# A hybrid decoder layer on one core: the small matrix products of the two token mixers, regrouped

## The chip, the cores and the metric

The kernel runs on one core of a Trainium2 chip. The metric is the device time of one execution in microseconds (us), lower is better; the times are medians over several runs. The core has a matrix engine (PE, whose weight loads are shown as PEld), a vector engine (DVE), a scalar engine (ACT), a general one (POOL), and queues that issue transfers (here almost all on SP).

## What is computed

One layer with two parallel token mixers, for 256 tokens (S) of 1024 channels, all in float32:

```python
n = rms_norm(h, norm1_g)
mq, mk, mv, gq, gk, gv, g_low, g_out, gate_moba, gate_gla = split(n @ w_in)
# MoBA: 8 heads of 64, one block of 256 keys: causal softmax attention
l_own = q @ k.T * scale + bias_hb[:, t5_bucket(d_own)]        # relative position bias
# GLA: 4 heads, dk = 128, dv = 256, chunks of 64 tokens
log_a = log_sigmoid(g_low @ gla_gate_up + gla_gate_bias) / 16  # g_low has 16 columns
attn = where(causal, (q * exp(b)) @ (k * exp(-b)).T, 0)        # b: cumulative sum of log_a in a chunk
mixed = sigmoid(gate_moba) * (y_moba @ w_branch_moba) + sigmoid(gate_gla) * (y_gla @ w_branch_gla)
h = h + mixed @ w_out
h = h + square(relu(rms_norm(h) @ w_up)) @ w_down
```

The weights are float32 and are read once; 78.74 MB are moved in all.

## The kernel before

**The large products.** Every large float32 product is made of three products of parts: an operand is split into a high part that is rounded to the type `float32r` and the low rest, and high x high, high x low and low x high are summed up in a PSUM bank. The weights come in units of 1 MB (`load`, L81). For each half of a unit ACT writes the high part (`wh`, L94) and, one step later, DVE the low part (`wl`, L98); when a unit's last low part is written, the transfer of the unit four further on is issued (L101). All of this runs two units ahead of PE (`split(hu + 2, ...)`). `block` (L118 to L120) multiplies 128 tokens by 512 columns, 4 x 3 products with 512 moving columns; `block_w` (L136 to L138) makes transposed results, 8 x 3 products with 256.

**The mixers' steps.** The projection is 26 units, each in two blocks; block number t of unit hu is slot 2 hu + t. A table of `at(slot, function)` (from L665) puts a small step of the mixers behind the slot's block. In every slot the order is written out: the block on PE, then `flush` (the deferred DVE halves of the slot before), then ACT's half of a weight split, then the results of the block, then the steps of the table in the order in which they were entered. Engines take their instructions in that order; nothing reorders them between engines. The results of the first two units (`mq`, `mk`) are entered as steps of slots 5 to 8, behind the table's own.

**The steps that the change touches:**
- `make_bias` (slot 7): one float32 product of 33 rows (32 buckets and a mask row), weights of 8 columns (`t5`) and 384 moving columns (`onehot`), both straight from transfers; bank `pbias`, L262. DVE copies the result (L264) and a transfer through memory spreads it.
- `g_diag`, `g_row` (slots 6 and 8): diag(rstd) by DVE (L459), then ones^T diag as one float32 product with 256 columns (bank `prow`, L466): the tokens' rstd in every row.
- `g_low` (slot 11): the 16 columns of the low-rank gate in 16 products with 256 columns; the weights `lowS` hold high, low, high, low parts, 64 columns (bank `plow`, L475 and L476). The result is split again into `lowHL`, 64 rows (L478 to L484).
- `g_decay` (two halves, slots 13 and 14): for each head 64 rows of `gup`'s high part by all of `lowHL` (L494), plus 32 rows of its low part by `lowHL`'s first 32 rows (L495), 256 columns each, bank `pz`.
- `m_transpose` (L316), `m_ptrans` (L395): four 128x128 transposes each on PE; `m_scores` (L326): for a pair of heads, which lie in rows 0 to 63 and 64 to 127, three products of parts for the one and then three for the other.
- `g_scores` (slots 38, 39): plain float32, for each head three products of a 128x128 tile of attention: L566 (all 128 keys by the first 64 queries), L567 (64 weight columns: the first chunk's keys by the last 64 queries) and L569 (64 weight columns: the second chunk's keys by the last 64 queries).

A plain float32 product is two MATMUL records in the profile, a `float32r` one is one. The names `128*64` in a row give rows x columns of the weights.

Of the kernel before, what the change touches and what calls it, by code (L numbers as in the profile page):

```python
# [19 lines left out]
S = 256  # L20
# [14 lines left out]
# Projection columns in units of 512, by their place in w_in, in the order that they are worked on.  # L35
# [6 lines left out]
# Columns of the packed per-partition vectors.  # L42
# [4 lines left out]
def block_kernel(ctx, tc, xT0_d, xT_d, x_d, vec_d, wlow_d, w_d, up_d, t5_d, onehot_d, out_d):  # L47
# [28 lines left out]
    # ---- weights: raw, then an exact split into two parts of 12 bits  # L76
# [26 lines left out]
    # The vector engine's half of a split is issued a step after the scalar engine's.  # L103
# [18 lines left out]
    def block_t(i, j, g, a, acc):  # L122
        """A transposed block: 128 columns of a unit that holds 256 for all of K, half of K, all tokens.
        The result is the sum of the bank's halves: those of the high and of the low parts in a."""
        for k in range(4):
            h, c = divmod(4 * g + k, 2)
            c = slice(c * 256 + j * P, c * 256 + (j + 1) * P)
            nc.tensor.matmul(acc, wH[i][:, h, c], a[:, k, :], start=g == 0 and k == 0, stop=False)  # L128
            nc.tensor.matmul(acc[:, S:], wL[i][:, h, c], a[:, k, :S], start=False, stop=g == 1 and k == 3)  # L129

    def block_w(i, j, g, aH, aL, acc):
        """The same, with the sum in one place."""
# [10 lines left out]
    # ---- first loads  # L143
# [19 lines left out]
    nc.vector.memset(t5[NB:NB + 1, :], 1.0)  # L163
    gup = mid("gup")
    ones = const.tile([P, P], F32, name="ones")
    nc.vector.memset(ones, 1.0)
    touch = const.tile([P, 1], F32, name="touch")
    nc.scalar.activation(touch, ones[:, 0:1], AF.Exp)

    # The tensor engine's clock rises while it works: keep it at work until the operands arrive.  # L170
# [18 lines left out]
    # ---- x^T times the gain, split  # L189
# [11 lines left out]
    def rsqrt(dst, ss, n):  # L201
        """dst = (ss / n + EPS) ** -0.5"""
# [15 lines left out]
    for r in range(4):  # L218
        nc.sync.dma_start(gup[16 * r:16 * r + 16, :], up_d)
# [19 lines left out]
    # The low-rank weights' columns: high, low, high, low parts; those that raise the rank: four copies  # L239
    T = {}  # L240
    lowS = const.tile([P, 8, 64], F32R, name="lowS")

    def low_split():
        v = lowS.rearrange("p k (r a c) -> p k r a c", r=2, a=2)
        for r in range(2):
# [4 lines left out]
    def gup_split():  # L250
        both = big("gupHL", F32R)
        T["gupH"], T["gupL"] = gupH, gupL = both[:64, :512], both[:32, 512:]
        nc.scalar.activation(gupH, gup[:64, :], AF.Copy)
        nc.vector.tensor_tensor(gupL, gup[:32, :], gupH[:32, :].bitcast(F32), op=OP.subtract)

    # ---- relative position bias: u[h, j] is the bias at distance 255 - j; bias[p, h, k] that of
    # query 128 + p and key k, which serves both tiles of queries
    bias = t4.tile([P, H, 256], F32, name="bias", tag="t8", bufs=2)

    def make_bias():  # L260
        pb = axbank("pbias")
        nc.tensor.matmul(pb[:H, :384], t5, onehot, start=True, stop=True)  # L262
# [5 lines left out]
    def spread_bias():  # L268
        """A copy for each partition, so that the row of partition p can start p elements earlier."""
# [13 lines left out]
    # ---- MoBA: one block of keys, so each query attends over its own block  # L283
# [40 lines left out]
    def m_scores(o, r, k, tq, tk):  # L324
        for i, (a, b) in enumerate(PARTS):
            nc.tensor.matmul(o, T["mq" + a][r, k, tq], T["mk" + b][r, k, tk], start=i == 0, stop=i == 2)  # L326

    def m_scores0():
        T["s0"] = big("s0").rearrange("p (k a c) -> p k a c", k=4, a=2)
        banks = [axbank(f"ps0{a}") for a in range(2)]  # L330
        for k in range(4):
            for a in range(2):
                r = slice(a * DH, (a + 1) * DH)
                m_scores(banks[a][:, k * P:(k + 1) * P], r, k, slice(0, P), slice(0, P))
# [5 lines left out]
    def m_scores1(half):  # L340
# [3 lines left out]
        for k in range(2):  # L344
            for a in range(2):
                r = slice(a * DH, (a + 1) * DH)
                m_scores(banks[a][:, k * S:(k + 1) * S], r, 2 * half + k, slice(P, S), slice(0, S))
# [25 lines left out]
    def m_weights(part):  # L373
        """The softmax's weights, from the exponentials."""
# [8 lines left out]
    def m_ptrans(part):  # L383
        """Transposes of the weights: heads 0-3 or 4-7 of query tile 0 (parts 0, 1), then of query
        tile 1 and keys 0-127 or 128-255 (parts 2-5)."""
# [24 lines left out]
    def m_av(k):  # L410
        """Of a pair of heads, transposed: both heads' values by each head's weights; the even head's
        result is in the upper rows of its columns, the odd head's in the lower ones."""
# [22 lines left out]
    def put_split(dH, dL, t, p, gain=None):  # L435
        """Splits a bank of four transposed tiles into the two parts, times a gain per row."""
# [18 lines left out]
    # ---- GLA  # L455
    def g_diag():
        T["diag"] = mid("diag")
        for t in range(NT):
            nc.vector.tensor_scalar(T["diag"][:, t * P:(t + 1) * P], ident, rstd[:, t:t + 1], None, op0=OP.mult)  # L459
# [3 lines left out]
    def g_row():  # L463
        """rstd of each token in all rows: ones^T diag(rstd)"""
        pr = axbank("prow")
        nc.tensor.matmul(pr[:, :S], ones, T["diag"][:, :S], start=True, stop=True)  # L466
        nc.scalar.activation(rrow, pr[:, :S], AF.Copy)

    def g_low():
        """The low-rank projection, transposed: rows 0-15 and 16-31 add up to it, and are there twice."""  # L470
        p = axbank("plow")
        o = p[:64, :S]
# [4 lines left out]
        low = mid("low")[:64, :S]  # L477
        nc.vector.tensor_tensor(low, o, rrow[:64, :], op=OP.mult)  # L478
        # Rows 0-31: the high part; rows 32-63: the low part
        both = t2.tile([P, 512], F32R, name="lowHL", tag="t2")  # L480
# [523 lines left out]
```

## Time and profile before

| | |
|---|---|
| median of 3 runs | 423.07 us (422.81 to 423.31) |
| the profiled execution: span from first to last instruction | 421.4 us |
| its own time beside the span | not recorded; the median is 1.67 us above the span |
| PE busy | 416.3 us, 99% of the span, 2160 products |
| PEld / DVE / ACT / POOL busy | 83% / 67% / 53% / 4% |
| mean granted clock of PE | 0.999 |
| transfers | 78.74 MB, 187 GB/s over the span |

Busy is the share of the span in which an engine had an instruction under way. Products overlap on PE, so a product's duration is longer than the time that it adds: what it adds is the distance from its start to the start of the next. Starts are the first number of a timeline row.

### The profile page before, as it was taken

The page shows a single profiled execution, that of the slowest core. Times are in us where ns is not written, and L with a number is a line of the kernel's source. Part 1 is how long each engine was busy: PE and PEld are TensorE (multiplying, and loading weights), DVE is VectorE, ACT ScalarE, POOL GpSimd, SP SyncE. Part 2 cuts the span into 40 slices and gives each one's busy share as a digit, 9 for nine tenths or more (in the row PEclk, how much of TensorE's full clock was granted, in tenths as well). Part 3 has the DMA queues.
Part 4 walks back from the last instruction along what each step waited for, and adds up shares of the span by engine and source line. Part 5 has one row for each costly group of instructions (what it writes and reads, how often), then busy time and mean ns, then how long its engine had stood idle before and what let it go on. Part 6 is the DMA issues. An engine that isn't in the chain of part 4 may idle for free.

```text
span 421.4 us, 5431 instructions
## 1 busy us (share of the span) xinstructions
PE 416.3 (99%) x2160; PEld 347.8 (83%) x2160; DVE 281.7 (67%) x359; ACT 221.3 (53%) x335; POOL 18.0 (4%) x22
## 2 busy tenths in 40 slices
PE   8999999999999999999999999999999999999996
PEld 4779988788888888888888888888888888888885
DVE  3759676889778652865665878748493838374752
ACT  5777465687845564562423456546452617263520
POOL 2025000000002011000000000000000000000000
PEclk9999999999999999999999999999999999999999
DMA  7987865354354243471765536726364554737002
GB/s 235 415 291 293 319 222 197 128 183 149 141 199 160 103 163 117 158 274 47 264 215 199 184 128 201 271 117 249 150 219 180 172 228 124 276 104 296 0 2 100
DMA packets 14581, 78.74 MB, mean 187 GB/s; under 512 B 1635, under 2 KB 3612, under 8 KB 6108
## 3 DMA queue, kind: packets, MB, share of 16 engines
q1 hardware_dynamic: 14236, 77.34, 51.6%
q10 hardware_dynamic: 288, 1.05, 0.8%
q8 instruction: 17, 0.28, 0.3%
q0 software_dynamic: 32, 0.01, 0.0%
q14 instruction: 8, 0.07, 0.0%
HBM read 77.33 MB, written 2.63 MB: 190 GB/s over the span
## 4 chain that ended last, share of the span: by engine, by line
PE 96%; DMA 1%; SPq 1%; DVE 1%; issue 0%; ACT 0%
PE pu L128 14%; PE acc L118 9%; PE acc L119 9%; PE acc L120 9%; PE pu L129 7%; PE fa L118 7%; PE fa L120 7%; PE fa L119 7%; PE acc L136 2%; PE acc L137 2%; PE acc L138 2%; PE po L118 2%; PE po L120 2%; PE pg L118 2%; PE po L119 2%; PE pg L120 2%
## 5 line engine op out<-in xcount | busy, mean ns | idle before, releaser
L98 DVE TENSOR_TENSOR wl<-raw,wh 128x1024 fp32r<-128x1024 f32 (+1 forms) x140 | 163.4, 1189 | 18.9 <-ACT wh L94 18.5
L94 ACT ACTIVATE wh<-raw 128x1024 fp32r<-128x1024 f32 (+1 forms) x140 | 140.1, 1027 | 24.1 <-PE pg L120 9.8
L128 PE MATMUL pu<-hHL,wh 128*128 128x512 f32 x256 | 90.9, 399 | 0.0
L129 PE MATMUL pu<-hHL,wl 128*128 128x256 f32 x256 | 71.9, 281 | 0.0
L118 PE MATMUL acc<-wh,xH 128*128 128x512 f32 x176 | 70.7, 402 | 0.1
L119 PE MATMUL acc<-wl,xH 128*128 128x512 f32 x176 | 69.1, 393 | 0.7 <-DVE wl L98 0.7
L120 PE MATMUL acc<-wh,xL 128*128 128x512 f32 x176 | 68.7, 390 | 0.0
L128 PEld LDWEIGHTS pu<-hHL,wh 128*128 128x128 f32 x256 | 48.1, 188 | 11.8
L129 PEld LDWEIGHTS pu<-hHL,wl 128*128 128x128 f32 x256 | 48.3, 189 | 0.3
L118 PE MATMUL fa<-wh,fH 128*128 128x512 f32 x124 | 48.5, 391 | 0.0
L120 PE MATMUL fa<-wh,fL 128*128 128x512 f32 x124 | 48.4, 390 | 0.0
L119 PE MATMUL fa<-wl,fH 128*128 128x512 f32 x124 | 48.3, 389 | 0.0
L854 ACT ACTIVATE half<-pu 128x256 f32<-128x256 f32 x32 | 12.0, 378 | 55.3 <-PE pu L129 55.3
L119 PEld LDWEIGHTS acc<-wl,xH 128*128 128x128 f32 x176 | 33.1, 188 | 8.1 <-DVE wl L98 2.1
L118 PEld LDWEIGHTS acc<-wh,xH 128*128 128x128 f32 x176 | 33.1, 188 | 7.9 <-ACT wh L94 1.3
L120 PEld LDWEIGHTS acc<-wh,xL 128*128 128x128 f32 x176 | 33.0, 188 | 7.0
L855 DVE TENSOR_TENSOR sq<-pu,half 128x256 f32<-128x256 f32 x32 | 13.4, 422 | 35.6 <-ACT half L854 35.5
L120 PEld LDWEIGHTS fa<-wh,fL 128*128 128x128 f32 x124 | 23.3, 188 | 5.1
L118 PEld LDWEIGHTS fa<-wh,fH 128*128 128x128 f32 x124 | 23.3, 188 | 4.9
L119 PEld LDWEIGHTS fa<-wl,fH 128*128 128x128 f32 x124 | 23.3, 188 | 4.7
L860 ACT ACTIVATE fH<-sq 128x512 fp32r<-128x512 f32 x16 | 10.1, 633 | 20.3 <-DVE sq L857 20.3
L136 PE MATMUL acc<-xH,wh 128*128 128x256 f32 x64 | 18.6, 291 | 0.0
(226 smaller groups left out, 533.1 us busy)
## 6 DMA issues: line engine op xcount, KB each, us to landing
raw<-w SPq DMA_DIRECT2D x65, 1024.0 KB, 5.0
raw<-w SPq DMA_DIRECT2D x8, 256.0 KB, 5.2
ur<-ud SPq DMA_DIRECT2D x1, 1536.0 KB, 9.8
raw<-w SPq DMA_DIRECT2D x2, 512.0 KB, 6.6
xs<-xs SPq DMA_DIRECT2D x2, 512.0 KB, 11.5
bias<-ur SPq DMA_DIRECT2D x1, 1024.0 KB, 8.8
xr<-xs ACTq DMA_DIRECT2D x2, 512.0 KB, 4.6
out<-o SPq DMA_DIRECT2D x3, 256.0 KB, 2.1
```

The costliest lines, as they stand in the source:

```text
L94: nc.scalar.activation(wH[i][:, s, :], raw[i][:, s, :], AF.Copy)
L98: nc.vector.tensor_tensor(wL[i][:, s, :], raw[i][:, s, :], wH[i][:, s, :].bitcast(F32), op=OP.subtract)
L118: nc.tensor.matmul(acc, aH[:, k, tk], h, start=start and k == 0, stop=False)
L119: nc.tensor.matmul(acc, aH[:, k, tk], low, start=False, stop=False)
L120: nc.tensor.matmul(acc, aL[:, k, tk], h, start=False, stop=stop and k == 3)
L128: nc.tensor.matmul(acc, wH[i][:, h, c], a[:, k, :], start=g == 0 and k == 0, stop=False)
L129: nc.tensor.matmul(acc[:, S:], wL[i][:, h, c], a[:, k, :S], start=False, stop=g == 1 and k == 3)
L136: nc.tensor.matmul(acc, wH[i][:, h, c], aH[:, k, :], start=g == 0 and k == 0, stop=False)
L137: nc.tensor.matmul(acc, wH[i][:, h, c], aL[:, k, :], start=False, stop=False)
L854: nc.scalar.activation(half, acc[:, S:], AF.Copy)
L855: nc.vector.tensor_tensor(o, acc[:, :S], half, op=OP.add)
L860: nc.scalar.activation(H, v, AF.Copy)
```

## The change

Five things are done, all inside the projection's stretch:

- **Bias.** A zeroed tile `biasS` of 128 rows holds `t5` rounded in rows 0 to 32 and its rest in rows 64 to 96, and `onehot` in both places. ACT writes the upper rows, DVE the lower ones, in slot 7, and `pbias` becomes one `float32r` product of 128 rows.
- **Rstd row.** `diag` is split into two parts (one more ACT and one more DVE instruction), and `prow` is two `float32r` products.
- **Decay.** `lowS` has 96 columns (three times high, low), `gup` is loaded six times instead of four, and `gup` and `lowHL` become stacks of 96 rows in which the pairs of parts stand under each other. Each head is one product; the first half moves from slot 13 to slot 12.
- **GLA scores.** L566 and L569 become one product with all 128 queries; L567 follows it into the upper 64 rows.
- **MoBA.** `m_scores` goes to and fro between the two heads of a pair, and the transposes are moved so that two groups of four stand in one slot.

```diff
+    biasS = const.tile([P, H + 384], F32R, name="biasS")
+    nc.gpsimd.memset(biasS.bitcast(F32), 0.0)
...
-    for r in range(4):
+    for r in range(6):
         nc.sync.dma_start(gup[16 * r:16 * r + 16, :], up_d)
...
-    lowS = const.tile([P, 8, 64], F32R, name="lowS")
+    lowS = const.tile([P, 8, 96], F32R, name="lowS")
...
     def gup_split():
-        both = big("gupHL", F32R)
-        T["gupH"], T["gupL"] = gupH, gupL = both[:64, :512], both[:32, 512:]
-        nc.scalar.activation(gupH, gup[:64, :], AF.Copy)
-        nc.vector.tensor_tensor(gupL, gup[:32, :], gupH[:32, :].bitcast(F32), op=OP.subtract)
+        T["gup"] = up = t2.tile([P, 512], F32R, name="gupHL", tag="t2")[:96]
+        nc.scalar.activation(up, gup[:96, :], AF.Copy)
+        nc.vector.tensor_tensor(up[64:], gup[64:96, :], up[64:].bitcast(F32), op=OP.subtract)
...
     def make_bias():
         pb = axbank("pbias")
-        nc.tensor.matmul(pb[:H, :384], t5, onehot, start=True, stop=True)
+        hi, lo = biasS[:NB + 1], biasS[64:64 + NB + 1]
+        nc.scalar.activation(hi[:, :H], t5, AF.Copy)
+        nc.vector.tensor_tensor(lo[:, :H], t5, hi[:, :H].bitcast(F32), op=OP.subtract)
+        nc.scalar.activation(hi[:, H:], onehot, AF.Copy)
+        nc.vector.tensor_copy(lo[:, H:], onehot)
+        nc.tensor.matmul(pb[:H, :384], biasS[:, :H], biasS[:, H:], start=True, stop=True)
...
-    def m_scores(o, r, k, tq, tk):
+    def m_scores(banks, cols, k, tq, tk):
...
         for i, (a, b) in enumerate(PARTS):
-            nc.tensor.matmul(o, T["mq" + a][r, k, tq], T["mk" + b][r, k, tk], start=i == 0, stop=i == 2)
+            for e in range(2):
+                r = slice(e * DH, (e + 1) * DH)
+                nc.tensor.matmul(banks[e][:, cols], T["mq" + a][r, k, tq], T["mk" + b][r, k, tk],
+                                 start=i == 0, stop=i == 2)
...
     def g_diag():
-        T["diag"] = mid("diag")
+        T["diag"] = d = t2.tile([P, 512], F32R, name="diag", tag="t2")
+        full = mid("diagf")[:, :S]
         for t in range(NT):
-            nc.vector.tensor_scalar(T["diag"][:, t * P:(t + 1) * P], ident, rstd[:, t:t + 1], None, op0=OP.mult)
+            nc.vector.tensor_scalar(full[:, t * P:(t + 1) * P], ident, rstd[:, t:t + 1], None, op0=OP.mult)
+        nc.scalar.activation(d[:, :S], full, AF.Copy)
+        nc.vector.tensor_tensor(d[:, S:], full, d[:, :S].bitcast(F32), op=OP.subtract)
...
-        nc.tensor.matmul(pr[:, :S], ones, T["diag"][:, :S], start=True, stop=True)
+        for a in range(2):
+            nc.tensor.matmul(pr[:, :S], ones, T["diag"][:, a * S:(a + 1) * S], start=a == 0, stop=a == 1)
...
-            nc.tensor.matmul(o, T["gupH"][:, hs], T["lowT"], start=True, stop=False)
-            nc.tensor.matmul(o, T["gupL"][:, hs], T["lowT"][:32], start=False, stop=True)
+            nc.tensor.matmul(p[:, j * S:(j + 1) * S], T["gup"][:, h * DK:(h + 1) * DK], T["low"],
+                             start=True, stop=True)
...
-            nc.tensor.matmul(p[:, o:o + CH], ki[:, b:b + P], q[:, b:b + CH], start=True, stop=True)
+            nc.tensor.matmul(p[:, o:o + P], ki[:, b:b + P], q[:, b:b + P], start=True, stop=True)
             nc.tensor.matmul(p[:CH, o + CH:o + P], kd[:, b:b + CH], q[:, b + CH:b + P],
                              start=True, stop=True)
-            nc.tensor.matmul(p[CH:, o + CH:o + P], ki[:, b + CH:b + P], q[:, b + CH:b + P],
-                             start=True, stop=True)
...
-    at(12, m_transpose, "mq", 0)
     at(12, m_norm, "mk", 1)
+    at(12, g_decay, 0)
+    at(13, m_transpose, "mq", 0)
     at(13, m_transpose, "mq", 1)
-    at(13, g_decay, 0)
     at(14, g_decay, 1)
-    at(14, m_transpose, "mk", 0)
     at(14, load_bias)
+    at(15, m_transpose, "mk", 0)
     at(15, m_transpose, "mk", 1)
...
-    at(28, m_ptrans, 0)
     at(29, g_exp, "edec")
+    at(29, m_ptrans, 0)
     at(29, m_ptrans, 1)
-    at(30, m_ptrans, 2)
+    at(31, m_ptrans, 2)
     at(31, m_ptrans, 3)
     at(31, g_qk, "eb")
-    at(32, m_ptrans, 4)
+    at(33, m_ptrans, 4)
     at(33, m_ptrans, 5)
```

The change moves instructions on three engines. First ACT, around slots 6 and 7. Before, the two halves of unit 5's split (`wh_328`) with the results of the first unit between them, and then the low-rank weights' split, each row with what its instruction waits for:

```order
L94 ACTIVATE wh_328<-raw_192 128x1024 [waits DMAHW3_49,DVE_49,PE_49]
L293 ACTIVATE mq<-acc_199,rstd 128x512
L295 ACTIVATE sq<-acc_199,rstd 128x512
L94 ACTIVATE wh_328<-raw_192 128x1024
L246 ACTIVATE lowS<-wlow 128x8x16 [waits DMAHW6_49]
```

Now, where the unit's high part is called `wh_332`:

```order
L94 ACTIVATE wh_332<-raw_196 128x1024 [waits DMAHW5_49,DVE_49,PE_49]
L469 ACTIVATE diag<-diagf 128x256 [waits DVE_49]
L301 ACTIVATE mq<-acc_203,rstd 128x512
L303 ACTIVATE sq<-acc_203,rstd 128x512
L94 ACTIVATE wh_332<-raw_196 128x1024
L266 ACTIVATE biasS<-t_105 33x8
L268 ACTIVATE biasS<-onehot 33x384 [waits DMAHW4_49]
```

One instruction (`diag`) has come between the two halves, and the two copies into `biasS` stand behind both of them.

DVE at the same place, now (`wl_333` is unit 5's low part), and the product on PE that stands behind slot 7's block, before and now:

```order
L470 TENSOR_TENSOR diag<-diagf,diag 128x256 [waits Activation_49]
L98 TENSOR_TENSOR wl_333<-raw_196,wh_332 128x1024 [waits DMAHW5_49,PE_49]
L308 TENSOR_REDUCE ssm<-sq 128x8 [waits Activation_49]
L208 TENSOR_SCALAR rsv<-ssm 128x8 [waits DVE_49]
L267 TENSOR_TENSOR biasS<-t_105,biasS 33x8 [waits Activation_49]
L269 CAST biasS<-onehot 33x384 [waits DMAHW4_49]
```

```order
L262 MATMUL pbias<-onehot,t_105 8x384 [waits DMAHW5_49,DMAHW4_49]
```

```order
L270 MATMUL pbias<-biasS 8x384 [waits DVE_49,Activation_49,Pool_49]
```

The product waited for two transfers before; it now waits for the last of ACT's and DVE's copies and for POOL's zeroes.

PE in slot 38, the scores of two heads, before and now (an f32 row of this list is two records of the profile):

```order
L566 MATMUL pa<-eb,einv 128x64
L567 MATMUL pa<-eb,edec 64x64
L569 MATMUL pa<-eb,einv 64x64
L566 MATMUL pa<-eb,einv 128x64
L567 MATMUL pa<-eb,edec 64x64
```

```order
L576 MATMUL pa<-eb,einv 128x128
L577 MATMUL pa<-eb,edec 64x64
L576 MATMUL pa<-eb,einv 128x128
L577 MATMUL pa<-eb,edec 64x64
```

The product with 64 weight columns still stands between any two with 128; the one that ran beside it is gone.

## Rows read from the trace of the kernel before

**Rows 1.** The page's chain of work that ended last, share of the span by engine.

```profile
PE 96%; DMA 1%; SPq 1%; DVE 1%; issue 0%; ACT 0%
```

**Rows 2.** PE's waits: waiting line, released by: us in total, times, longest us.

```profile
PE acc L119 <- DVE wl L98: 0.7, 3, 0.2
```

**Rows 3.** Timeline of PE around `pbias`: start us, us, line, out<-in, weights, moving operand, count.

```profile
29.10 0.39 PE L119 MATMUL acc<-wl,xH 128*128 128x512 f32 x1
29.32 0.39 PE L120 MATMUL acc<-wh,xL 128*128 128x512 f32 x1
29.64 0.81 PE L262 MATMUL pbias<-onehot,t 33*8 33x384 f32 x2
30.38 0.38 PE L136 MATMUL acc<-xH,wh 128*128 128x256 f32 x1
30.60 0.28 PE L137 MATMUL acc<-xL,wh 128*128 128x256 f32 x1
```

**Rows 4.** Timeline of PE around `prow`.

```profile
33.35 0.59 PE L466 MATMUL prow<-diag,ones 128*128 128x256 f32 x2
```

**Rows 5.** Timeline of PE around `plow`.

```profile
42.29 0.28 PE L138 MATMUL acc<-xH,wl 128*128 128x256 f32 x1
42.41 0.28 PE L475 MATMUL plow<-xH,lowS 128*64 128x256 f32 x1
```

**Rows 6.** Timeline of PE around `pz`, first and second half.

```profile
50.95 0.38 PE L494 MATMUL pz<-lowHL,gupHL 64*128 64x256 f32 x1
51.26 0.38 PE L495 MATMUL pz<-lowHL,gupHL 32*128 32x256 f32 x1
...
52.41 0.28 PE L137 MATMUL acc<-xL,wh 128*128 128x256 f32 x1
...
55.04 0.28 PE L138 MATMUL acc<-xH,wl 128*128 128x256 f32 x1
...
56.49 0.66 PE L316 MATMUL pt<-ident,mk 128*128 128x128 f32 x4
```

**Rows 7.** Timeline of PE in the GLA scores: second head of the first tile.

```profile
134.58 0.43 PE L566 MATMUL pa<-eb,einv 128*128 128x64 f32 x2
134.95 0.27 PE L567 MATMUL pa<-eb,edec 128*64 128x64 f32 x1
134.95 0.27 PE L569 MATMUL pa<-eb,einv 128*64 128x64 f32 x1
...
135.21 0.43 PE L566 MATMUL pa<-eb,einv 128*128 128x64 f32 x2
```

**Rows 8.** Timeline of PE: plain float32 products with 128 columns and 128 weight columns.

```profile
144.59 1.05 PE L584 MATMUL pax<-gx 128*128 128x128 f32 x8
```

**Rows 9.** Timeline of PE in the MoBA scores of the second tile.

```profile
73.25 0.29 PE L326 MATMUL ps<-mkL,mqH 64*128 64x256 f32 x2
```

**Rows 10.** Timeline of ACT from slot 6's split on; in brackets idle before and releaser.

```profile
29.57 1.06 ACT L94 ACTIVATE wh<-raw 128x1024 fp32r<-128x1024 f32 x1 [1.56 <-DMA raw<-w]
...
31.68 1.06 ACT L94 ACTIVATE wh<-raw 128x1024 fp32r<-128x1024 f32 x1
32.62 0.50 ACT L246 ACTIVATE lowS<-wlow 128x128 fp32r<-128x128 f32 x2
```

**Rows 11.** Timeline of SP: the transfers of units 5, 6 and 7.

```profile
24.59 1.30 SPq L85 DMA_DIRECT2D raw<-w  x3
```

**Rows 12.** Timeline of DVE in slot 7.

```profile
32.54 0.17 DVE L205 TENSOR_SCALAR rsv<-ssm 128x8 f32<-128x8 f32 x1
32.62 0.54 DVE L264 COPY u<-pbias 8x384 f32<-8x384 f32 x1
```

**Rows 13.** Timelines of DVE and PE where the decay is moved to.

```profile
45.82 0.41 DVE L484 TENSOR_TENSOR lowHL<-low,lowHL 32x256 fp32r<-32x256 f32 x1 [0.97 <-ACT lowHL L483]
47.11 0.27 PE L316 MATMUL pt<-ident,mq 128*128 128x128 f32 x1
```

**Rows 14.** Timeline of PE at the start, seven products with 512 columns.

```profile
0.85 3.15 PE L174 MATMUL pwarm<-const-bfloat16-1.0 128*128 128x512 bf16 x7 [0.85 <-PEq L996]
```

More of the change, by code (lines that the diff above doesn't have):

```diff
@@ L163, in block_kernel @@
     nc.vector.memset(t5[NB:NB + 1, :], 1.0)
+    biasS = const.tile([P, H + 384], F32R, name="biasS")
+    nc.gpsimd.memset(biasS.bitcast(F32), 0.0)
     gup = mid("gup")
-    ones = const.tile([P, P], F32, name="ones")
-    nc.vector.memset(ones, 1.0)
+    ones = const.tile([P, P], F32R, name="ones")
+    nc.vector.memset(ones.bitcast(F32), 1.0)
     touch = const.tile([P, 1], F32, name="touch")
-    nc.scalar.activation(touch, ones[:, 0:1], AF.Exp)
+    nc.scalar.activation(touch, ones[:, 0:1].bitcast(F32), AF.Exp)
     pw = axbank("pwarm")
@@ L240, in block_kernel @@
     T = {}
-    lowS = const.tile([P, 8, 64], F32R, name="lowS")
+    lowS = const.tile([P, 8, 96], F32R, name="lowS")
     def low_split():
-        v = lowS.rearrange("p k (r a c) -> p k r a c", r=2, a=2)
-        for r in range(2):
+        v = lowS.rearrange("p k (r a c) -> p k r a c", r=3, a=2)
+        for r in range(3):
             nc.scalar.activation(v[:, :, r, 0, :], wlow, AF.Copy)
@@ L331, in m_scores0 @@
         for k in range(4):
-            for a in range(2):
-                r = slice(a * DH, (a + 1) * DH)
-                m_scores(banks[a][:, k * P:(k + 1) * P], r, k, slice(0, P), slice(0, P))
+            m_scores(banks, slice(k * P, (k + 1) * P), k, slice(0, P), slice(0, P))
         bv = bias.rearrange("p (k a) c -> p k a c", a=2)
@@ L344, in m_scores1 @@
         for k in range(2):
-            for a in range(2):
-                r = slice(a * DH, (a + 1) * DH)
-                m_scores(banks[a][:, k * S:(k + 1) * S], r, 2 * half + k, slice(P, S), slice(0, S))
+            m_scores(banks, slice(k * S, (k + 1) * S), 2 * half + k, slice(P, S), slice(0, S))
         bv = bias.rearrange("p (k a) c -> p k a c", a=2)
@@ L471, in g_low @@
         p = axbank("plow")
-        o = p[:64, :S]
+        o = p[:96, :S]
         for kt in range(8):
@@ L476, in g_low @@
             nc.tensor.matmul(o, lowS[:, kt, :], xL[g][:, k, :], start=False, stop=kt == 7)
-        low = mid("low")[:64, :S]
-        nc.vector.tensor_tensor(low, o, rrow[:64, :], op=OP.mult)
-        both = t2.tile([P, 512], F32R, name="lowHL", tag="t2")
-        T["lowT"], high = both[:64, :S], both[:64, S:]
-        nc.scalar.activation(T["lowT"][:32], low[:32], AF.Copy)
-        nc.scalar.activation(high[32:], low[32:], AF.Copy)
-        nc.vector.tensor_tensor(T["lowT"][32:], low[32:], high[32:].bitcast(F32), op=OP.subtract)
+        low = mid("low")[:96, :S]
+        nc.vector.tensor_tensor(low, o, rrow[:96, :], op=OP.mult)
+        T["low"] = both = t2.tile([P, 512], F32R, name="lowHL", tag="t2")[:96, :S]
+        nc.scalar.activation(both, low, AF.Copy)
+        nc.vector.tensor_tensor(both[32:64], low[32:64], both[32:64].bitcast(F32), op=OP.subtract)
     def g_decay(half):
@@ L491, in g_decay @@
             h = 2 * half + j
-            hs = slice(h * DK, (h + 1) * DK)
-            o = p[:, j * S:(j + 1) * S]
-            nc.tensor.matmul(o, T["gupH"][:, hs], T["lowT"], start=True, stop=False)
-            nc.tensor.matmul(o, T["gupL"][:, hs], T["lowT"][:32], start=False, stop=True)
+            nc.tensor.matmul(p[:, j * S:(j + 1) * S], T["gup"][:, h * DK:(h + 1) * DK], T["low"],
+                             start=True, stop=True)
         for j in range(2):
```

## The prediction

> **What bounds the kernel now.** I read the chain of waits first: 96% of the span is PE [rows 1]. The list of PE's waits then says that after its first steps PE waits for almost nothing: 0.7 us in three waits of at most 0.2 [rows 2]. So whatever PE does less comes off the time, and whatever it is made to wait goes on, unless an engine that fills PE's operands becomes late. Third I read timelines of PE for the price of each small product, by distances between starts: a product with 512 columns adds 0.22 to 0.23 us [rows 3], one with 256 columns 0.12 [rows 5]. Fourth, the timelines of ACT and DVE around slot 7, because the change lets PE wait for them there.
>
> Around slot 7 ACT is behind PE. PE starts the last large product of slot 7's block at 29.32, and could go on at 29.32 + 0.23 = 29.55 [rows 3]. ACT at that moment has not begun slot 6's split of unit 5: it sat idle for 1.56 us until that unit's transfer landed and starts at 29.57; slot 7's split follows at 31.68, and what stands behind it starts at 32.62 [rows 10]. Before, nobody felt this: PE needs unit 5 only in slot 10, and `pbias` took its operands from transfers.
>
> **The change on PE.** The sum is made against the profiled execution's span, 421.4 us; its own time is not recorded, and the median of 423.07 is 1.67 above that span, which I keep.
>
> - Bias: from 29.32 to 30.60 PE needs 1.28 us; 0.23 and 0.12 of it are the large products on both sides, so the bias costs 0.93 [rows 3]. One product with 384 columns at 0.12 per 256 is 0.18. Saved: 0.75; if its 8 weight columns still cost a change of the array's layout on both sides, some 0.1 each, 0.55.
> - Rstd row: two records in 0.59 us, the last of which is as long as a lone product with 256 columns, so about 0.21 each [rows 4]. Two products at 0.12 instead save 0.2. DVE and ACT make the parts in slot 6 for slot 8.
> - Decay: in the second half from 55.04 to 56.49 there is one large product and four of `pz`: 1.45 - 0.12 = 1.33; in the first from 50.95 to 52.41: 1.46 - 0.12 = 1.34 [rows 6]. Each starts 0.31 after the one before, since 64 and 32 rows take turns. Two halves are 2.67, with the boundary that the rows leave out on one side of each 2.8. Four products of 96 rows at 0.12 are 0.5. Saved: 2.3. If 96 rows cost a change of layout as 64 and 32 do, 4 x 0.31 and the boundaries remain and 1.3 is saved. I take 2.3: `plow`, with 64 of 128 weight columns, starts 0.12 after its neighbour as if nothing had changed [rows 5], and with 96 rows no smaller layout is left to use.
>
>   The Trainium skill, page "TensorEngine Tiling (Array Packing)", section "Key Properties", says that changing the tiling mode drains TensorE. The `pz` rows agree, the `plow` row does not; by that sentence the bias product would pay twice, and the saving on PE would be 0.2 smaller.
> - `g_low`: 96 weight columns for 64, 16 products. Between nothing and 0.1 in all; I take 0.05.
> - Scores: a head takes 135.21 - 134.58 = 0.63 us. L569 starts with L567, at 134.95, so leaving it out frees almost nothing [rows 7]. L567 still stands between two products with all columns, so the two changes of layout per head stay. The other product's two records get 128 columns for 64; at 128 columns a record adds 1.05 / 8, some 0.12 [rows 8], at 64 half of that. Dearer per head by at least 0 (the second weight load covers it) and at most 2 x 0.06; I take 0.05, since one of the two streams can hide beside a load: 8 x 0.05 = +0.4.
> - MoBA: the pairs already run side by side, two products in the 0.29 us that one takes [rows 9], so taking turns is worth 0. Grouping the transposes: costed at nothing; it removes boundaries that show no wait. The decay in slot 12 needs `lowHL`, which DVE finished at 45.82 + 0.41 = 46.23, before PE comes to that place at 47.11 [rows 13]; were that cover gone, at most the difference would be waited for.
>
> PE's work: -0.75 - 0.2 - 2.3 + 0.05 + 0.4 = **-2.8 us**, between -1.6 and -3.3.
>
> **The wait that is added.** `pbias` now needs two ACT copies and two DVE copies of slot 7. ACT's stand behind both halves of unit 5's split. Before, the place behind them came up at 32.62 [rows 10]. Two things push it back. The two more transfers of `gup` stand on SP ahead of unit 5's; SP spends 1.30 / 3 = 0.43 on each issue [rows 11], so that unit starts up to 0.87 later; I take 0.75, as an issue may partly wait anyway. And the copy of `diag`, 256 elements, has come in between: two copies of 128 take 0.50 [rows 10], so 0.3. ACT begins `biasS` at 32.62 + 0.75 + 0.3 = 33.67. The first, tiny copy takes at most the 0.25 of a 128-element one; DVE's subtraction follows, 0.17 as for another tiny one, then its copy of 384 elements, 0.54 as for `u` of the same length [rows 12]: 33.67 + 0.2 + 0.17 + 0.54, about 34.6. ACT's own copy of 384 elements ends by then. PE stands from 29.55 to 34.6: **+5.0 us**. At the least, with the transfers where they were and the copies at half their price, it is 32.62 + 0.3 + 0.5 = 33.4, or 3.9; at the most, with all 0.87 and slow handovers, 5.6.
>
> Queued behind it on PE are slot 8's block and all that follows; DVE's copy of `u` waits with it. Nothing on PE later waits long enough to give this back [rows 2]. ACT, DVE and the transfers gain five microseconds of lead, so their other additions (a third copy of `lowS`, POOL's zeroes at the start) cost nothing.
>
> **The clock.** The page shows a granted clock of 0.999 in this run, and PE never stands for long in it. What PE does after having stood shows only at the start: its first seven products with 512 columns took 3.15 us [rows 14], which is the 1.2 GHz level; at the later 0.23 they take 1.6. So the loss lies between 0 and 1.6 if the same happens once. I take 0.6, below the middle, because no row shows a fall after a gap as short as 5 us.
>
> The sum: 421.4 - 2.8 + 5.0 + 0.6 = 424.2 of span, with 1.67 around it **425.9 us**.
>
> **Rivals.**
>
> *The wait is covered, and the change is faster.* The place is the end of slot 7's block; were `biasS` ready when PE comes there, only PE's saving is left: 423.07 - 2.8 = 420.3. It decides at a wait of 2.8 us: under that the change gains. For it: three of the four copies need nothing but data that landed long ago. Against it: engines work in their written order, and ACT is held by unit 5's transfer until 29.57 already. 6%.
>
> *The scores lose their changes of layout.* Without L569 only the first columns of the array are used, as in `plow`; if that is then as free as in `plow` [rows 5], a head falls from 0.63 to about 4 x 0.06 + 0.1, and eight save some 2.4 where I added 0.4: 425.9 - 2.8 = 423.1, no change. Against it: L567 itself is unchanged, and the row behind the 128-column product shows the delay at L567 as much as at L569. 6%.
>
> *The clock falls and stays down longer.* Then the whole loss of the start comes on, or twice that: 425.3 + 1.6 = 426.9 to 425.3 + 3.2 = 428.5. For it: a standstill of 5 us is far longer than any that this run has once its blocks are under way. Against it: no row of this run shows a fall. 24%, of which I put 10% beyond 427.9. The page "TensorE: Matmul & The Clock Gate" of the Trainium skill, section "Why this matters for your kernels", warns against idle gaps between bursts of products, since the clock falls back; no run here shows it yet.
>
> **How the numbers follow.** The forecast has 64%, the rivals 6, 6 and 24. The range takes the smaller wait and larger saving at its low end (423.07 - 3.0 + 4.2 = 424.3, a little less) and the lower clock for the start's length with the longer wait at its high end (423.07 - 2.5 + 5.6 + 1.6 = 427.8): 424.1 to 427.9. A measurement tells 0.2%, some 0.85 us, from no change. Faster by more: 7%. Within it: 7%, from the second rival and the lowest wait. Slower by more: 86%.
>
> **What would show it.** Right: PE idle for about 5 us before `pbias`, released by DVE's copy into `biasS`; four `pz` products 0.12 apart; a head's scores at 0.63 to 0.75; the MoBA pairs as before. Products behind the gap with the double distance would show the clock. Wrong: `pbias` right behind slot 7's block, `pz` at 0.31, or scores at 0.35 a head.

## The result, and the profile after

| | before | after |
|---|---|---|
| median | 422.94 us (4 runs, 422.55 to 423.31) | 426.48 us (4 runs, 426.24 to 426.83) |
| ratio, 95% interval | | 1.0082 (1.0069 to 1.0094) |
| profiled execution: time / span | not recorded / 421.4 us | 426.46 / 424.7 us |
| PE busy | 416.3 us | 414.7 us |
| mean granted clock of PE | 0.999 | 0.991 |

The changed kernel is slower by 0.8%. PE is busy for 1.6 us less by the table (products at a lower clock count longer there), and the span is 3.3 us longer, so PE stands or crawls somewhere. The chain of waits says it first; the line that was 96% PE [rows 1] now reads:

```profile
PE 91%; DMA 6%; ACT 1%; SPq 0%; issue 0%; DVE 0%; ACTq 0%
```

Six per cent of the span now hang on transfers, although no large transfer was added: the chain runs from PE over ACT back to the transfer of a weight unit. The list of PE's waits (waiting line, released by: us in total, times, longest), which had 0.7 us [rows 2], names the place:

```profile
PE pbias L270 <- ACT lowS L250: 4.8, 1, 4.8
PE pwarm L177 <- PEq L1004: 0.8, 1, 0.8
PE acc L119 <- DVE wl L98: 0.4, 2, 0.2
PE acc L118 <- ACT wh L94: 0.4, 1, 0.4
```

It is one wait. The timeline of PE there (start us, us, instruction, in brackets idle before and releaser) answers to [rows 3]:

```profile
28.99 0.39 PE L120 MATMUL acc<-wh,xL 128*128 128x512 f32 x1
34.19 0.48 PE L270 MATMUL pbias<-biasS 128*8 128x384 f32 x1 [4.82 <-ACT lowS L250]
34.47 0.41 PE L136 MATMUL acc<-xH,wh 128*128 128x256 f32 x1
...
38.31 0.30 PE L136 MATMUL acc<-xH,wh 128*128 128x256 f32 x1
38.44 0.28 PE L137 MATMUL acc<-xL,wh 128*128 128x256 f32 x1
```

Two things are to be seen. PE could have gone on at 28.99 + 0.23 = 29.22 and goes on at 34.19: it stands 4.97 us. Then, from 34.47 to 38.31, 18 products with 256 columns start 0.213 apart, where the same ones stand 0.12 apart later: 3.84 - 18 x 0.12 = 1.68 us lost after the stand. A view of stretches shows that this is the clock (stretch: its length, busy us and instructions of PE, PEld, DVE, ACT and POOL, granted clock, share of transfers, GB/s):

```profile
29.20:34.20 5.00, 0.18 (x2) 0.04 (x2) 2.79 (x6) 4.41 (x10) 1.55 (x2) 0.73 1.01 426
34.20:38.30 4.10, 4.10 (x19) 4.10 (x20) 3.56 (x9) 2.26 (x4) 1.36 (x2) 0.50 0.69 249
38.30:42.30 4.00, 4.00 (x35) 4.00 (x35) 1.62 (x3) 2.83 (x5) 2.54 (x2) 1.00 0.63 246
```

The granted clock is 0.50 in the whole second stretch, the 1.2 GHz level, and 1.00 in the third: 19 products where 35 fit.

ACT and DVE in the same time answer to [rows 10, 12]:

```profile
29.80 1.06 ACT L94 ACTIVATE wh<-raw 128x1024 fp32r<-128x1024 f32 x1 [2.27 <-DMA raw<-w]
...
32.20 1.05 ACT L94 ACTIVATE wh<-raw 128x1024 fp32r<-128x1024 f32 x1
33.15 0.20 ACT L266 ACTIVATE biasS<-t 33x8 fp32r<-33x8 f32 x1
33.25 0.51 ACT L268 ACTIVATE biasS<-onehot 33x384 fp32r<-33x384 f32 x1
```

```profile
33.59 0.16 DVE L267 TENSOR_TENSOR biasS<-t,biasS 33x8 fp32r<-33x8 f32 x1
33.67 0.38 DVE L269 CAST biasS<-onehot 33x384 fp32r<-33x384 f32 x1
```

ACT stands idle for 2.27 us until unit 5's transfer has landed, does both halves of its split with `diag` and the results of a block between them, and only then the copies. DVE's copy is the last, done at 34.05; PE starts 0.14 later. The list of waits names `lowS` as the releaser, the instruction that ACT had under way then; by the program the product waits for nothing behind the copies. A releaser in such a list is a guess that the order has to confirm.

What was saved is there too. PE at the low-rank gate, the decay's first half, and two heads of the GLA scores, for [rows 5, 6, 7]:

```profile
47.90 0.28 PE L488 MATMUL plow<-xH,lowS 128*96 128x256 f32 x1
...
49.78 0.28 PE L136 MATMUL acc<-xH,wh 128*128 128x256 f32 x1
...
52.66 0.40 PE L503 MATMUL pz<-lowHL,gupHL 96*128 96x256 f32 x2
52.90 0.28 PE L136 MATMUL acc<-xH,wh 128*128 128x256 f32 x1
...
138.07 0.33 PE L577 MATMUL pa<-eb,edec 128*64 128x64 f32 x2
...
138.74 0.33 PE L577 MATMUL pa<-eb,edec 128*64 128x64 f32 x2
```

Half the decay costs 0.24 us where it cost 1.33; 96 rows change nothing on the array. A head's scores take 138.74 - 138.07 = 0.67 where they took 0.63; over the two tiles that is 0.37 more (2.41 and 2.42 before, 2.60 each now). The MoBA pairs still run two products side by side:

```profile
76.46 0.28 PE L337 MATMUL ps<-mkL,mqH 64*128 64x256 f32 x2
76.58 0.28 PE L337 MATMUL ps<-mkH,mqL 64*128 64x256 f32 x2
```

They were side by side before [rows 9], so taking turns has nothing to give.

### The profile page after: what moved, and what is told of

It reads as the page before. It is cut to its first block, busy times and chain, and to the rows that moved or that the text cites. A ratio compares the mean times of both kernels' runs of the same rounds, so it can differ in the third digit from the quotient of the medians.

```text
span 424.7 us, 5399 instructions
## 1 busy us (share of the span) xinstructions
PE 414.7 (98%) x2139; PEld 348.5 (82%) x2139; DVE 283.4 (67%) x363; ACT 222.1 (52%) x338; POOL 18.0 (4%) x23
## 4 chain that ended last, share of the span: by engine, by line
PE 91%; DMA 6%; ACT 1%; SPq 0%; issue 0%; DVE 0%; ACTq 0%
PE pu L128 14%; PE acc L118 8%; PE acc L119 8%; PE acc L120 8%; PE pu L129 7%; PE fa L118 7%; PE fa L120 7%; PE fa L119 7%; DMA raw<-w 3%; DMA xs<-xs 3%; PE acc L137 2%; PE acc L136 2%; PE acc L138 2%; PE po L120 2%; PE po L118 2%; PE pg L118 2%
```

## The experiments

The theory after the result: all of the loss is the one wait, 4.97 us of standing and some 1.7 of low clock behind it; it comes from ACT's order (copies behind unit 5's split) and from the transfer that holds that split; everything else in the change is a saving of about 2 us. The rivals were that PE would have had to wait for unit 5 anyway, that the extra transfers of `gup` are the cause, and that the slow stretch is something else than the answer to the standstill. Ratios below are to the kernel before, measured on the same chip. Its median was 422.91 us beside the first four runs, 423.45 beside the next four (*bias_slot8*, *gup_late*, *decay13*, *scores_grouped*) and 422.98 beside the last two, so runs of different groups are compared by their ratios.

### The bias product undone, and alone

*bias_undone* is the change with the old bias product:

```diff
-        hi, lo = biasS[:NB + 1], biasS[64:64 + NB + 1]
...
-        nc.tensor.matmul(pb[:H, :384], biasS[:, :H], biasS[:, H:], start=True, stop=True)
+        nc.tensor.matmul(pb[:H, :384], t5, onehot, start=True, stop=True)
```

> The change, but with the bias product as before (plain float32, straight from the transfers, no copies, no zeroed tile). Theory (a wait of 5.0 us for the copies, then some 1.6 us of products at the lower clock, everything else of the change is a saving): both go, the product costs 0.93 again: 426.5 - 5.0 - 1.6 + 0.5 = 420.4 us, PE's waits below 1 us. Rival (PE would wait anyway, since unit 5 is late and slot 10 needs its parts): the wait reappears at slot 10 and the time stays above 423.

Measured: 420.93 us, ratio 0.9948 (0.9936 to 0.9961). The chain is 96% PE again, and PE's waits after the start are down to 0.4 us in two. So the wait did not come back at unit 5, and the rest of the change is worth 2.0 us (422.91 to 420.93): the rstd row, the decay, `g_low` and the scores make 0.2 + 2.3 - 0.06 - 0.37 = 2.1 by the rows above. The grouped transposes of the softmax's weights give 0.18 more, 2.3 in all: from the end of the MoBA scores to the first `py`, PE takes 35.68 us before (83.26 to 118.94) and 35.50 after (86.46 to 121.96). The profiled execution, 420.51, meets the expectation of 420.4; the median is 0.5 above it, and why the other executions are longer is not recorded.

*bias_alone* is the kernel before with the bias part alone (the zeroed tile, the four copies, the float32r product).

> The kernel before, with the bias part of the change alone. Theory: ACT is held by unit 5's transfer here too, so PE stands before the product, but without the copy of diag (0.3) and the two more transfers ahead of unit 5 (0.23 by its start on ACT): about 4.1 to 4.4 us; if the clock falls after that too, 1.6 more: 422.9 + 4.2 + 1.6 - 0.5 = 428.2 us. If a stand of 4 us leaves the clock up: 426.6. Rival (the stand comes mostly from the two more transfers): a wait under 2 us and a time under 425.

Measured: 427.92 us, ratio 1.0112 (1.0093 to 1.0130). This part alone loses 5.0 us. PE stands without `diag` and without the two extra transfers too, for 3.4 us of idle time (3.55 by the starts, as the 4.97 was counted), so the rival that blames the transfers falls: they don't make the wait. That they lengthen it is tried with gup_late. The profiled execution is the fastest of the four (426.82), and its wait is shorter than the 4.1 to 4.4 expected; how long PE stood in the others is not recorded. The clock falls here as well, but not at once. PE's timeline after the stand:

```profile
32.53 0.34 PE L269 MATMUL pbias<-biasS 128*8 128x384 f32 x1 [3.39 <-ACT lowS L248]
...
33.53 0.33 PE L137 MATMUL acc<-xL,wh 128*128 128x256 f32 x1
33.66 0.41 PE L138 MATMUL acc<-xH,wl 128*128 128x256 f32 x1
...
37.06 0.59 PE L473 MATMUL prow<-diag,ones 128*128 128x256 f32 x2
```

PE works on at 2.4 GHz for 1.1 us, and then goes at 1.2 GHz until 37: 16 products take 37.06 - 33.66 = 3.40 us instead of 16 x 0.12, so the fall costs about 1.5 us. The price is paid late, on products that wait for nothing.

### The same stand, but filled

*bias_filled* is the change with 18 useless products in the place of the standstill, of which 1.4 us are left:

```diff
+        for _ in range(18):
+            nc.tensor.matmul(pb, warm[:, :P], warm, start=True, stop=True)
         nc.tensor.matmul(pb[:H, :384], biasS[:, :H], biasS[:, H:], start=True, stop=True)
```

> The change, with 18 dummy bf16 products of 512 columns (4.1 us at 0.227) ahead of the bias product, into its own bank, so that PE is busy while the copies are made. Theory (the standstill itself lets the clock fall): the product starts when it did, 34.2, but the products behind it stay at 0.12 us: 426.5 - 1.6 = 424.9 us, granted clock 0.999. Rival (the clock falls for another reason at this time, or the slow stretch is not the clock): 426.5.

Measured: 425.56 us, ratio 1.0060 (1.0046 to 1.0074), clock 0.999 to 1.000 in its executions. PE after the wait:

```profile
34.84 0.34 PE L272 MATMUL pbias<-biasS 128*8 128x384 f32 x1 [1.39 <-ACT lowS L250]
35.01 0.28 PE L136 MATMUL acc<-xH,wh 128*128 128x256 f32 x1
35.13 0.28 PE L137 MATMUL acc<-xL,wh 128*128 128x256 f32 x1
```

The products stand 0.12 apart, so the slow stretch is the clock's answer to the idle array. By the medians the filling gives back 0.9 us, 0.7 less than expected. In the profiled execution (425.24) the product started at 34.84, not at 34.19: unit 5's split began at 30.44, 0.64 later than after's 29.80. That start differs from one profile to the next; it is looked at below. If the other executions were as late, the filling gives back some 1.6 us, an estimate.

*bias_slot8* leaves the copies in slot 7 and moves the product behind slot 8's block, so that the stand becomes shorter.

> The change, with the four copies left in slot 7 and the product moved behind the block of slot 8. PE then has slot 8's 24 products (2.9 us) to do while the copies are made; they are done near 34.1 (later or earlier with unit 5's transfer), so about 2 us of standing are left. If so short a stand leaves the clock up: 426.5 - 2.9 - 1.6 = 422.0 us. If it falls as after 5.0 and 3.5 us: 423.6.

Measured: 424.02 us median, 422.40 to 424.66 in 12 runs, ratio 1.0006 (0.9995 to 1.0018). Neither number: the executions differ. Six have a granted clock of 0.994 to 0.996 and lie between 423.97 and 424.66 (median 424.15). Six have 0.999 or 1.000: five of them lie between 422.40 and 423.17, and the sixth, the profiled one, at 424.07. In it PE stood for 2.4 us, and the clock did not fall behind the stand, as the list of waits and a view of stretches show:

```profile
PE pbias L272 <- ACT lowS L250: 2.4, 1, 2.4
```

```profile
37.60:40.60 3.00, 3.00 (x27) 3.00 (x27) 2.97 (x5) 3.00 (x6) 1.34 (x2) 1.00 0.76 240
```

That execution is long for another reason. Its first weight units came late (ACT waits 1.43 us for one at 15.53, where it waits 0.26 at 13.51 in after), and PE ended slot 7's block at 31.13 for after's 29.22:

```profile
31.13 0.28 PE L136 MATMUL acc<-xH,wh 128*128 128x256 f32 x1
```

How long PE stood in the others is not recorded. So the 1.2 us between the six and the five are a fall of the clock together with whatever their stands differ by. What the runs tell: after a stand of this kind the clock falls in some executions and not in others.

### Where the wait comes from

SP's order explains unit 5. In this program an issue waits not only for a free buffer, but for a semaphore that the transfer eight places earlier in the queue raises when it lands. The rows of the changed program's SP that wait for number 3 (output of the instruction list, not of the profile):

```
L217 DMA xs_166<-xs 128x1024 [waits DMAHW3_49]
...
L222 DMA gup<-gup 16x512 [waits DMAHW3_49]
L222 DMA gup<-gup 16x512 [waits DMAHW4_49]
L85 DMA raw_196<-w 128x2048 [waits DMAHW5_49,DVE_49]
```

The second half of `xs` raises number 3. The fifth load of `gup` waits until that half has landed, and unit 5 stands behind it. The traces agree. ACT's first use of that half, and SP, in the profile of after:

```profile
24.07 1.06 ACT L235 ACTIVATE junk<-xs 128x1024 f32<-128x1024 f32 x1 [0.59 <-DMA xs<-xs]
```

```profile
24.06 0.78 SPq L222 DMA_DIRECT2D gup<-gup  x2
24.93 0.37 SPq L85 DMA_DIRECT2D raw<-w  x1
```

In the kernel before, unit 5 itself was the eighth behind `xs`, and SP issued it at 24.59 [rows 11], right after that half's first use at 24.55:

```profile
24.55 1.06 ACT L232 ACTIVATE junk<-xs 128x1024 f32<-128x1024 f32 x1 [0.88 <-DMA xs<-xs]
```

So unit 5 is issued 0.86 behind that use where it was 0.04: two more loads push it by 0.82 against the landing of `xs`. bias_alone, with four loads, agrees (23.72 and 23.76). That landing itself moves from one profile to another.

*gup_late* issues all six loads in slot 4's steps, where they stand behind units 5 to 7:

```diff
-    for r in range(6):
-        nc.sync.dma_start(gup[16 * r:16 * r + 16, :], up_d)
...
+    def load_gup():
+        for r in range(6):
+            nc.sync.dma_start(gup[16 * r:16 * r + 16, :], up_d)
...
+    at(4, load_gup)
```

> The change, with the six transfers of gup issued in slot 4's steps, behind those of units 5 to 7. Theory (ACT's late start on unit 5 is the transfer's, which waits in SP's order behind the transfers of gup and through them for those of xs): unit 5 is there before ACT comes to it at 27.4, the copies are done near 31.7, PE stands some 2.5 us: 424.0 us with a fall of the clock, 422.4 without. Rival (the transfers are bound by memory and unit 5 lands late anyway): unit 5's split still begins after 29 us, and the time stays within 0.5 of 426.5.

Measured: 424.41 us, 422.32 to 425.86 in 11 runs, ratio 1.0021 (1.0007 to 1.0036). SP issues unit 5 eight microseconds earlier, and ACT comes to its split without waiting for it (no idle time stands in the first row):

```profile
16.53 6.34 SPq L85 DMA_DIRECT2D raw<-w  x3
```

```profile
27.76 1.06 ACT L94 ACTIVATE wh<-raw 128x1024 fp32r<-128x1024 f32 x1
29.21 0.42 ACT L471 ACTIVATE diag<-diagf 128x256 fp32r<-128x256 f32 x1 [0.39 <-DVE diagf L470]
```

The theory's expectation holds, with 3.0 us of standing for 2.5 (ACT now waits 0.39 for `diagf` instead). Of the 4.8 us about 1.8 were the transfer's, 3.0 are ACT's own order. These shares are from one profile of each. Eight of the 11 executions have a clock of 0.994 to 0.996, the profiled one among them, and lie between 423.82 and 425.86 (median 424.6); three have 0.999 and lie between 422.32 and 423.77 (median 423.3). Again some executions pay for the stand twice and some do not.

### The copies moved ahead

*bias_early* keeps the float32r product in slot 7 and enters the copies as a step of slot 5, ahead of unit 5's split:

```diff
-    def make_bias():
-        pb = axbank("pbias")
+    def copy_bias():
...
+    def make_bias():
+        pb = axbank("pbias")
...
+    at(5, copy_bias)
     at(7, make_bias)
```

> The change, with the four copies into the product's tile entered as a step of slot 5, ahead of unit 5's split, and the product left in slot 7. Theory: the copies are done near 27 us, before PE is at the end of slot 7's block at 29.2; no wait, no fall of the clock, product 0.2 to 0.4 us: 419.7 to 420.0 us. Rival (the wait moves on to unit 5's parts, or slot 5 delays what follows): above 421.

Measured: 420.77 us, ratio 0.9945 (0.9932 to 0.9958). The wait is gone, and the product costs what a float32r product with 384 columns costs:

```profile
29.59 0.34 PE L272 MATMUL pbias<-biasS 128*8 128x384 f32 x1
29.77 0.28 PE L136 MATMUL acc<-xH,wh 128*128 128x256 f32 x1
```

That is 0.18 us for the 0.93 of [rows 3]; eight weight columns cost no change of layout. But the time is 0.8 above the expectation, and no better than with the old product. With the stand gone, the next late things show, in a profiled execution of 421.32:

```profile
32.64 0.82 PE L480 MATMUL prow<-diag,ones 128*128 128x256 f32 x2
33.30 0.28 PE L136 MATMUL acc<-xH,wh 128*128 128x256 f32 x1
...
47.43 0.50 PE L505 MATMUL pz<-lowHL,gupHL 96*128 96x256 f32 x2 [0.59 <-DVE lowHL L497]
47.77 0.28 PE L136 MATMUL acc<-xH,wh 128*128 128x256 f32 x1
```

The rstd row takes 33.30 - 32.64 = 0.66 for two products of 0.12: the parts of `diag` come late, since its copy on ACT stands behind unit 5's split as the bias copies did, and that split begins only at 31.20 here. (In the profiles of decay13 and scores_grouped, which have the same order there, it begins at 30.51 and 30.87, and the row takes 0.24: this wait does not come in every execution.) And the decay, moved from slot 13 to slot 12, now comes before DVE has finished `lowHL`. In the changed kernel the five microseconds of standing had covered both. The rival is right in part: some of the wait moves on, through unit 5's split.

*decay13* is bias_early with the decay's first half back in slot 13.

> bias_early, with the first half of the decay back in slot 13 (behind the eight transposes). Theory (without the stand PE comes to slot 12 before DVE has lowHL; there it waits 0.85 us for it): the wait goes, 420.8 - 0.85 = 419.9 us, and the two halves cost 0.24 each. Rival (all of PE is early against DVE there): the wait comes back at the next block.

Measured: 420.20 us, ratio 0.9922 (0.9909 to 0.9934). By the ratios that is 1.0 less than bias_early (0.57 by the medians) for 0.85 expected, with intervals that touch. The wait before the decay is gone, and a part, 0.27, is paid at the MoBA scores, as the rival has it: the second pair starts 0.44 after the first, and in bias_early (61.21 and 61.38) it was 0.17.

```profile
60.02 0.33 PE L339 MATMUL ps<-mkH,mqH 64*128 64x128 f32 x2
60.46 0.33 PE L339 MATMUL ps<-mkL,mqH 64*128 64x128 f32 x2
```

It waits for `mkL`, whose first half DVE began at 59.66 and took 0.74 for.

### The scores in groups

The change keeps a product with 64 weight columns between any two with 128. *scores_grouped* is bias_early with the four products of L576 first and the four of L577 after them:

```diff
             nc.tensor.matmul(p[:, o:o + P], ki[:, b:b + P], q[:, b:b + P], start=True, stop=True)
+        for h in range(GH):
+            b, o = h * S + t * P, h * P
             nc.tensor.matmul(p[:CH, o + CH:o + P], kd[:, b:b + CH], q[:, b + CH:b + P],
```

> bias_early, with the four products of L576 of a tile first and then the four of L577. Theory (between 64 and 128 weight columns of plain float32 the array changes over, some 0.1 us on either side of each L577): two changes a tile instead of eight; a tile falls from 2.72 to between 1.5 and 1.95 us: 420.8 - 2.0 = 418.8, between 418.3 and 419.2 us. Rival (a product with 64 weight columns costs its 0.15 to 0.2 itself, whatever stands beside it): 420.8.

Measured: 418.83 us, ratio 0.9888 (0.9873 to 0.9904), as expected; by the ratios 2.4 below bias_early. A tile's scores:

```profile
131.60 1.05 PE L578 MATMUL pa<-eb,einv 128*128 128x128 f32 x8
132.59 0.68 PE L581 MATMUL pa<-eb,edec 128*64 128x64 f32 x8
133.19 0.50 PE L118 MATMUL acc<-wh,xH 128*128 128x512 f32 x1
```

From 131.60 to 133.19 are 1.59 us; in the changed kernel the same sixteen records took 139.68 - 137.08 = 2.60 (the expectation has 2.72). The order alone is worth 1.0 us a tile, 2.0 in all: the cost was the changing over, not the products.

### All together

*combined* is bias_early with `diag` also in slot 5, the loads of gup_late and the grouped scores; *combined13* has the decay's first half in slot 13 besides.

> The change with all that the runs so far suggest: copies into the bias tile and diag in slot 5, gup's transfers behind those of units 5 to 7 (issued in slot 4), scores grouped as four and four. Theory: no wait at the bias product, at the rstd row or at slot 12's decay, since unit 5's split is no longer held by its transfer; scores 2.0 us cheaper: from scores_grouped's 418.8 the waits of 0.8 at the decay and 0.5 at a block go too: 417.6 us, PE's waits below 1 us after the start. Rival (DVE is late for slot 12's decay by its own work, not through unit 5): the wait before the decay stays, 418.3 us.

> The same with the first half of the decay in slot 13 behind the transposes, as in decay13. Theory: no difference from combined beyond 0.2 us, 417.6, as there is no wait left to dodge. Rival (slot 12 waits for DVE in combined): faster than combined by 0.5 or more.

Measured: 417.97 us, ratio 0.9882 (0.9866 to 0.9899), and 418.04 us, ratio 0.9886 (0.9871 to 0.9901). They are the same, as the theory has it, and the wait before the decay is gone with unit 5's transfer, not by moving the decay. In combined PE waits for this after the start:

```profile
PE acc L119 <- DVE wl L98: 0.7, 3, 0.2
PE acc L118 <- ACT wh L94: 0.3, 1, 0.3
```

The version is 1.2% faster than the kernel before and 2% faster than the changed one. It is 0.4 above the expectation, which is not explained further. Against scores_grouped the ratios differ by 0.3 us, well inside their intervals (0.9 by the medians, which are of different chips): that `diag` in slot 5 and the later loads gain time over it is not shown, only that the 0.5 us of waiting before its decay is gone from the profile.

## Why the prediction was right, and where it was not

Forecast 425.9 us within 424.1 to 427.9, slower with 86%; measured 426.48. The main step held, and one term was too small; that the total is only 0.6 off is partly luck, as the balance shows.

- **The wait.** Forecast 5.0 us, measured 4.97, and for the reason given: copies behind both halves of unit 5's split, and the split held by its transfer. Two parts of it were off and cancelled. ACT reached `biasS` at 33.15, not at 33.67, as `xs` was there earlier in that execution (24.07 for 24.55), and PE was there 0.33 earlier than in the profile of before. The 0.75 for the two loads is 0.82 against the landing of `xs`. What I had missed is why unit 5 waits there at all: the semaphore of the eighth transfer before it. The kernel before had that wait already, covered.
- **The clock.** This is the term that was mis-sized: 0.6 forecast; measured 1.68 on the 18 products behind the stand and 0.1 on the bias product itself. The sentence "I take 0.6, below the middle, because no row shows a fall after a gap as short as 5 us" was the wrong choice. Absence of a row was no evidence, as nothing in the profile of before had ever stood for so long; the only row that showed an array after idling, the start, gave 1.6, and that was nearly the value. So the mechanism of the third rival came true at its lower end, beside the forecast's wait; the time stayed under its 426.9 for the reasons under the balance. One reading behind the 1.6 goes further than its row: that the start runs at the 1.2 GHz level rests on the doubled distance of the products alone, as the view of stretches of the kernel before gives a granted clock of 1.00 there.

```profile
0.80:4.30 3.50, 3.45 (x9) 1.25 (x10) 0.71 (x3) 1.99 (x3) 2.75 (x8) 1.00 0.61 167
```

The Trainium skill, page "TensorE: Matmul & The Clock Gate", section "Why this matters for your kernels", warns against just such gaps between bursts; after and bias_alone agree with it, and in bias_filled, with the gap mostly filled, the clock stayed at 0.999 or above.

- **PE's savings.** Forecast 2.8. By the rows: bias 0.93 to 0.18 (seen at the full clock in bias_early), the decay's halves 1.33 each to 0.24, which with the boundary is the 2.3 (18.90 us from the end of `g_low` to the MoBA scores before, 16.57 after); the rstd row 0.2; `g_low` 1.88 us from 47.90 to 49.78 where it was about 1.82, so 0.06 dearer for 0.05; the scores 0.37 dearer in all for 0.4; the MoBA scores nothing; the transposes, costed at nothing, 0.18. That makes 3.0. In time: bias_undone is 2.0 below before, for 2.3 by the rows without the bias's 0.75.
- **Balance.** 421.4 - 2.8 + 4.97 + 1.8 = 425.4 of span, measured 424.7. Of the 0.7 between them, 0.33 is that PE came to slot 7 earlier: its waits for `wl` in the first 12 us differ from one profile to the next, and the cause of that was not tried. Another 0.2 is the saving, 3.0 for 2.8; the last 0.1 is open. So the clock's 1.2 us too little met 0.7 too much elsewhere, most of it chance.
- **Covers.** "Were that cover gone, at most the difference would be waited for" was said of `lowHL` and slot 12. While the stand was there nothing showed; in bias_early, without it, PE waited 0.59 there, as said, and in that execution also 0.42 for `diag` in slot 8, which was not named: its copy stands in the same queue behind the same split as the bias's.
- **The rivals.** "The wait is covered" is what combined makes of it on purpose. "The scores lose their changes of layout" did not come about with the change's order, but the price that it rested on is real: grouping the two kinds of products took 2.0 us off. The float32r products with 96 weight columns (`plow`) and with 8 (`pbias`) pay nothing of the kind: 0.12 and 0.18 us. The Trainium skill, page "TensorEngine Tiling (Array Packing)", section "Key Properties", says that a change of the tiling mode drains TensorE; the scores agree with that sentence, if 64 weight columns are another mode, and these two do not. Why plain float32 with 64 columns pays and float32r with 64 ([rows 5]) does not, no run here tells; their moving operands differ too, 64 columns and 256.

## What to carry to other kernels

A product that used to read transfers directly and now reads copies has joined the queues of the engines that copy: look at what stands ahead of the copies in those queues at that moment, and put preparation ahead of the first instruction that waits for a late transfer. A standstill of some microseconds on PE is paid once as the wait and, in some or all executions, a second time: 1.5 us in bias_alone and 1.8 in the changed kernel of products at the lower clock. Sort small products by shape before merging them: here four and four gave 2.0 us, and merging without sorting lost 0.37.

## What the runs showed that was not expected

- The fall of the clock need not lie in the stand: in bias_alone (3.4 us of standing) it came 1.1 us after PE had resumed, and the view of stretches has it at full, then at half. gup_late shows the same (1.00 from 32.70 to 33.80, 0.50 from 33.90 to 37.00); in the changed kernel it had fallen before the stand ended (0.50 from 31.60 to 34.20).

```profile
32.50:33.60 1.10, 1.07 (x9) 1.10 (x10) 0.70 (x3) 1.10 (x4) 1.02 (x1) 1.00 0.97 410
33.70:36.90 3.20, 3.20 (x17) 3.20 (x17) 3.17 (x6) 1.12 (x2) 0.90 (x1) 0.50 0.76 245
```

- With a stand of 2.4 to 3.0 us in the profiled execution, the clock falls in some executions of the same kernel and not in others (6 of 12 in bias_slot8, 8 of 11 in gup_late). The medians of the two groups are some 1.2 to 1.3 us apart when the late profiled execution of bias_slot8 is left out, but one execution at the full clock can be as long as one with a fall.
- In this program an issue on SP is tied to the landing of the transfer eight places before it: two loads of 32 KB moved a 1 MB transfer by 0.82 us, and taking six of them out of its way let it start 8 us earlier (16.53 for 24.93).
